# The beginning of each MLP: activations' forms made in steps beside the projection's last columns and the first products

## The chip, the cores and the metric

One core of one Trainium2 chip runs the whole program. TensorE (PE in the rows) does matmuls and transposes, VectorE (DVE) and ScalarE (ACT) the elementwise work, GpSimd (POOL) little here, and SyncE (SP) issues the loads of the weights. The metric is the device time of one execution in microseconds (us), the median of several runs.

## The reference

`x` has 256 tokens of width 2048. Everything is float32; the kernel gets that accuracy from TensorE by splitting each operand into a high and a low part.

```python
h = x
h = h + dsa_mixer(rmsnorm(h), a_w_in, a_w_out)        # top-64 keys of an indexer, then GQA; ends in "@ w_out"
h = h + sq_relu_mlp(rmsnorm(h, mlp_norm[0]), w_up[0], w_down[0])
k_sh, v_sh = shared K/V from rmsnorm(h, kv_norm) @ w_kv
h = h + dilated_mixer(rmsnorm(h), b_w_q, b_w_out, k_sh, v_sh)   # ends in "@ w_out" too
h = h + sq_relu_mlp(rmsnorm(h, mlp_norm[1]), w_up[1], w_down[1])
out = rmsnorm(h, final_norm)

def sq_relu_mlp(h, w_up, w_down):          # w_up 2048 x 8192, w_down 8192 x 2048
    u = jax.nn.relu(h @ w_up)
    return (u * u) @ w_down
```

## The kernel before

**Order of the program.** The kernel is a Python program that emits instructions for each engine; each engine runs its own in the order in which they were emitted or statically scheduled by the framework, and waits on semaphores where it needs another's result. Tiles come from pools with a fixed number of buffers; a new tile waits until the readers of the tile that had its buffer are through.

**A product.** Weights are loaded by `load_w` (L367) or `raws` (L699) as `wraw` tiles of 128 x 2 x 1024, one DMA of 1,024 KB each, issued in order on SP's queue. `split` (L190, L191) makes of each 1024 columns a high part `whi` (a cast on ScalarE) and a low part `wlo` (a subtraction on VectorE). TensorE then multiplies the activations' high part by both and their low part by the high part: three matmuls of 128 x 512 for each block (`gemm`, L389; `mm3`, L194 to L196). A step of `gemm` on 1024 columns is 12 such matmuls, after which `pump` takes some units from a queue of waiting work (generators handed over by `enqueue`); `flush` runs what is left.

**The projection.** `project` multiplies the heads' output by the second weight of the attention, in two column halves of 1024, and adds the result to the residual `h` (L652). The first `cut` of the 16 steps (8 in the first layer, 14 in the second) run for both halves while the last heads of attention are still finished beside them; then the `mlp` pool is opened, and the remaining steps run for each half in turn ("first columns", "second columns"), each with its own residual adds and the sums of squares for the norm (L331, ScalarE).

**The forms.** The MLP's first matrix product, `h @ w_up`, is computed block by block (`up(e)`, e from 0 to 7, 1024 columns each) as one 2 x 2 Strassen-like step with seven products on part of the depth and plain products on the rest. Its left operands are seven sums and differences of the activations' quarters (a11, a12, a22, s1 to s4), each split into high and low. `add_forms` makes them from `h`, half by half of the width: TensorE transposes `h` into a side bank (L299; there are two side banks), ScalarE copies and scales them (L307 for the plain part of half 0, L313 into a buffer `gx` that is taken from the weights' raw buffers), VectorE makes the low parts (L308) and sums (L316 to L319), and each form is split (L190, L191). It is called behind each half's columns:

```python
        for n in range(2):
            gemm(stat, range(cut, KC), w, 0, (n * GW, n * GW + HALF), residual(st, n))
            add_forms(forms, n, gain_next)
```

**The first block of the MLP.** `up(0)` loads two tiles of plain rows, computes two plain blocks (`plain(0, 0)`, `plain(0, 1)`), then three groups of seven products (`seven`), with two more plain blocks near the end. In a group of seven, VectorE also makes the weights' sums and differences in place, in the raw tiles (L731, L733, L735, L738). The results are combined from the eight accumulator banks (L746 to L765), and later transposed (L400) for the second matrix. During attention there are 3 raw, 4 high and 3 low weight buffers; the `mlp` pool adds 3 raw, 1 high and 2 low.

Of the kernel before, what the change touches and what calls it, by code (L numbers as in the profile page):

```python
# [11 lines left out]
F32 = mybir.dt.float32  # L12
# [80 lines left out]
def yoco_kernel(ctx: ExitStack, tc: tile.TileContext, x, a_w_in, a_w_out, w_kv, b_w_q, b_w_out, w_up, w_down,  # L93
# [13 lines left out]
    def open_scope(*names):  # L107
        if scope[0] is not None:
            scope[0].close()
        scope[0] = ExitStack()  # L110
        pools.clear()
        for n in names:
            pools[n] = scope[0].enter_context(tc.tile_pool(name=n, bufs=1))

    open_scope("keep", "att")
# [111 lines left out]

    def hi_lo():

        hi_of, lo_of = wp, wp  # L230
        if "mlp" in pools:
# [9 lines left out]
    def raw_tile():  # L241

        of = wp
        if "mlp" in pools:
# [46 lines left out]
    def add_forms(halves, half, which):  # L291
# [23 lines left out]
        s1, s2, s3, s4 = (b2()[:, :n * P].rearrange("p (q t) -> p q t", t=P) for _ in range(4))  # L315
        nc.vector.tensor_tensor(s1, a21, a22, op=ALU.add)  # L316
        nc.vector.tensor_tensor(s2, a11, s1, op=ALU.subtract)
        nc.vector.tensor_tensor(s3, a11, a21, op=ALU.subtract)
        nc.vector.tensor_tensor(s4, a12, s2, op=ALU.add)  # L319
        for name, v in (("a11", a11), ("a12", a12), ("s4", s4), ("s1", s1), ("s3", s3), ("s2", s2), ("a22", a22)):  # L320
            split(f[name][:, :, 0], f[name][:, :, 1], v)

# [48 lines left out]
    def gemm(stat, ks, w, row0, cols, evac, width=HALF, before=None, first_raw=None):  # L371
# [637 lines left out]
```

## Time and profile before

| | us |
|---|---|
| median of 3 runs | 2241.14 (2239.53 to 2241.89) |
| the profiled execution, its own time | 2240.57 |
| its span in the trace | 2238.6 |
| TensorE busy | 2176.6 |
| VectorE busy | 1692.6 |
| ScalarE busy | 1294.3 |

All stretches below are in microseconds from the start of the span. Rows of the table by stretches give the stretch, its length, the busy time of PE, PE's weight loads, DVE, ACT and POOL (each with the number of instructions), then the mean granted clock of TensorE as a share of full speed, the DMA engines' busy share and GB/s. Rows of the timeline give start, duration, engine, line, operation, out<-in with shape, the number of like instructions, and in brackets the idle time before them with what ended it. Rows of the waits give who waited for whom: total us, number of waits, the longest.

### The profile page before, as it was taken

The page shows a single profiled execution, that of the slowest core. Times are in us where ns is not written, and L with a number is a line of the kernel's source. Part 1 is how long each engine was busy: PE and PEld are TensorE (multiplying, and loading weights), DVE is VectorE, ACT ScalarE, POOL GpSimd, SP SyncE. Part 2 cuts the span into 40 slices and gives each one's busy share as a digit, 9 for nine tenths or more (in the row PEclk, how much of TensorE's full clock was granted, in tenths as well). Part 3 has the DMA queues.
Part 4 walks back from the last instruction along what each step waited for, and adds up shares of the span by engine and source line. Part 5 has one row for each costly group of instructions (what it writes and reads, how often), then busy time and mean ns, then how long its engine had stood idle before and what let it go on. Part 6 is the DMA issues. An engine that isn't in the chain of part 4 may idle for free.

```text
span 2238.6 us, 27840 instructions
## 1 busy us (share of the span) xinstructions
PE 2176.6 (97%) x10310; PEld 1792.3 (80%) x10310; DVE 1692.6 (76%) x2267; ACT 1294.3 (58%) x1736; POOL 99.5 (4%) x118
## 2 busy tenths in 40 slices
PE   9999988899999999999999999987999999999998
PEld 7788866688888888888888888865788888888886
DVE  5877749978878878866577777757979879779765
ACT  6545545656666666656455554445666666656563
POOL 0000000010010010110000000000010110100100
PEclk9999988999999999999999999998999999999999
DMA  8554534576676776674555445535477677777673
GB/s 301 162 178 150 162 139 146 174 226 227 207 231 224 208 225 238 206 244 136 173 163 162 156 156 162 185 121 181 164 222 248 194 228 241 207 226 242 204 250 95
DMA packets 164105, 434.44 MB, mean 194 GB/s; under 512 B 12800, under 2 KB 62080, under 8 KB 163968
## 3 DMA queue, kind: packets, MB, share of 16 engines
q1 hardware_dynamic: 146688, 401.25, 52.9%
q0 software_dynamic: 16128, 29.37, 7.4%
q10 hardware_dynamic: 1152, 2.04, 0.3%
q8 instruction: 81, 1.33, 0.2%
q14 instruction: 56, 0.46, 0.1%
HBM read 401.15 MB, written 2.10 MB: 180 GB/s over the span
## 4 chain that ended last, share of the span: by engine, by line
PE 90%; DVE 6%; ACT 2%; issue 1%; DMA 0%; DVEq 0%; ACTq 0%
PE acc L389 59%; PE acc L195 6%; PE acc L196 5%; PE acc L194 5%; PE side L195 4%; PE side L194 4%; PE side L196 4%; DVE wlo L191 2%; PE side L400 2%; ACT whi L190 1%; DVE wraw L733 1%; DVE wraw L735 0%; DMA wraw<-in_w_up_dram 0%; ACT b L331 0%; DVE wraw L731 0%
## 5 line engine op out<-in xcount | busy, mean ns | idle before, releaser
L190 ACT CAST whi<-wraw 128x1024 fp32r<-128x1024 f32 (+2 forms) x925 | 928.0, 1020 | 786.9 <-PE acc L389 510.1
L191 DVE TENSOR_TENSOR wlo<-wraw,whi 128x1024 fp32r<-128x1024 f32 (+2 forms) x925 | 1072.9, 1181 | 370.1 <-ACT whi L190 251.0
L389 PE MATMUL acc<-whi,xt 128*128 128x512 f32 x4160 | 1109.2, 380 | 7.7 <-ACT whi L190 7.7
L389 PEld LDWEIGHTS acc<-whi,xt 128*128 128x128 f32 x4160 | 739.7, 189 | 147.5 <-ACT whi L190 10.1
L389 PE MATMUL acc<-wlo,xt 128*128 128x512 f32 (+1 forms) x2080 | 619.2, 379 | 0.4 <-DVE wlo L191 0.4
L389 PEld LDWEIGHTS acc<-wlo,xt 128*128 128x128 f32 x2080 | 372.8, 188 | 75.4 <-DVE wlo L191 2.3
L649 POOL DMA_DIRECT2D h<-b x112 | 98.8, 1223 | 2094.1 <-ACT b L648 2076.0
L194 PE MATMUL side<-whi,xt 128*128 128x512 f32 x320 | 124.9, 400 | 15.2 <-ACT whi L190 14.4
L194 PE MATMUL acc<-whi,xt 128*128 128x512 f32 x328 | 129.3, 399 | 4.9 <-ACT whi L190 4.9
L195 PE MATMUL side<-wlo,xt 128*128 128x512 f32 x320 | 127.9, 400 | 0.8 <-DVE wlo L191 0.8
L195 PE MATMUL acc<-wlo,xt 128*128 128x512 f32 x328 | 127.9, 390 | 0.0
L196 PE MATMUL acc<-whi,xt 128*128 128x512 f32 x328 | 127.7, 389 | 0.0
L196 PE MATMUL side<-whi,xt 128*128 128x512 f32 x320 | 127.1, 397 | 0.0
L194 PE MATMUL acc<-whi,xf 128*128 128x512 f32 x288 | 114.9, 400 | 3.8 <-ACT whi L190 3.5
L195 PE MATMUL acc<-wlo,xf 128*128 128x512 f32 x288 | 115.0, 399 | 1.1 <-DVE wlo L191 1.1
L196 PE MATMUL acc<-whi,xf 128*128 128x512 f32 x288 | 112.9, 392 | 0.0
L194 PEld LDWEIGHTS side<-whi,xt 128*128 128x128 f32 x320 | 61.1, 192 | 30.7 <-ACT whi L190 16.9
L400 PE MATMUL side<-ident,b 128*128 128x128 f32 x512 | 77.1, 273 | 6.1 <-ACT b L773 4.9
L194 PEld LDWEIGHTS acc<-whi,xt 128*128 128x128 f32 x328 | 62.1, 190 | 22.1 <-ACT whi L190 9.8
L400 PEld LDWEIGHTS side<-ident,b 128*128 128x128 f32 x512 | 62.1, 140 | 21.4 <-ACT b L773 6.2
L195 PEld LDWEIGHTS side<-wlo,xt 128*128 128x128 f32 x320 | 61.6, 192 | 16.2 <-DVE wlo L191 2.0
L648 ACT ACTIVATE b<-acc,ri 128x512 f32<-128x512 f32 x112 | 71.0, 686 | 4.1
(194 smaller groups left out, 1738.3 us busy)
## 6 DMA issues: line engine op xcount, KB each, us to landing
wraw<-in_w_up_dram SPq DMA_DIRECT2D x128, 1024.0 KB, 6.4
wraw<-in_w_down_dram SPq DMA_DIRECT2D x128, 1024.0 KB, 6.6
wraw<-in_b_w_q_dram SPq DMA_DIRECT2D x192, 256.0 KB, 3.1
wraw<-in_a_w_in_dram SPq DMA_DIRECT2D x31, 1024.0 KB, 5.3
h<-b POOLq DMA_DIRECT2D x112, 256.0 KB, 7.7
wraw<-in_a_w_out_dram SPq DMA_DIRECT2D x16, 1024.0 KB, 5.7
wraw<-in_b_w_out_dram SPq DMA_DIRECT2D x16, 1024.0 KB, 5.5
wraw<-in_w_kv_dram SPq DMA_DIRECT2D x8, 1024.0 KB, 5.0
```

The lines of the kernel that those rows point to most:

```text
L190: nc.scalar.copy(hi, src)
L191: nc.vector.tensor_tensor(lo, src, hi.bitcast(F32), op=ALU.subtract)
L194: nc.tensor.matmul(o, a_hi, b_hi, start=start, stop=False)
L195: nc.tensor.matmul(o, a_hi, b_lo, start=False, stop=False)
L196: nc.tensor.matmul(o, a_lo, b_hi, start=False, stop=stop)
L389: nc.tensor.matmul(acc[t][i][:, :c1 - c0], stat(k, a, t), b[:, c0:c1], start=first and a == 0 and b is hi, stop=last and a == 1)
L400: nc.tensor.transpose(pt[:, j * P:(j + 1) * P], sr, ident)
L648: nc.scalar.activation(part, acc, AF.Copy, scale=scale()[:, t:t + 1])
L649: nc.gpsimd.dma_start(hh, part, accum_op=ALU.add)
L733: nc.vector.tensor_tensor(b12, b22, b12, op=sub)
```

## The change

`add_forms` becomes `form_steps`, which does nothing at once but returns two lists of steps: `on_pe` (transposes and copies) and `rest` (sums and splits). The sums come in another order, each followed by its split. `project` hands half 0's steps to the queue, spread over 8 steps of the second columns, so they are emitted between those columns' products; half 1's `on_pe` steps run behind the second columns, and its `rest` goes to the MLP as `late`, where the first group of seven of block 0 takes one step at each of its two hooks and the remaining ones behind it. `up(0)` runs three plain blocks ahead of the groups of seven, not two, and gives `q1` and `q6` the side banks. In the second layer (`again` is False) the cut is gone: the first columns run all 16 steps, with the heads finished (`heads_done`) before step 14, and the second columns run all 16 behind them. The residual adds run column by column. `gx` now always takes one of the `mlp` pool's 3 raw buffers, and the larger number of weight buffers (`more`) is used only from the start of `mlp` on.

```diff
-    def add_forms(halves, half, which):
+    def form_steps(halves, half, which):
...
-        if plain is not None:
-            for c in range(2):
-                for cc, pt, g in transposed(2 * half + c, 1):
-                    hi, lo = plain[:, 2 * c + cc - 2, 0, :], plain[:, 2 * c + cc - 2, 1, :]
-                    nc.scalar.activation(hi, pt, AF.Copy, scale=g)
-                    nc.vector.scalar_tensor_tensor(lo, pt, g, hi.bitcast(F32), op0=ALU.mult, op1=ALU.subtract)
-        gx = raw_tile()[:, :, :n * SEQ].rearrange("p c (j t) -> p c j t", t=SEQ)
-        for c in range(2):
-            for c2 in range(n // 2):
-                for cc, pt, g in transposed(2 * half + c, c2):
-                    nc.scalar.activation(gx[:, c, cc], pt, AF.Copy, scale=g)
+        gx = pools["mlp"].tile([P, 2, GW], F32, name="wraw", bufs=RAW_MORE)
+        gx = gx[:, :, :n * SEQ].rearrange("p c (j t) -> p c j t", t=SEQ)
...
+        def take(c, c2):
+            for cc, pt, g in transposed(2 * half + c, c2):
+                nc.scalar.activation(gx[:, c, cc], pt, AF.Copy, scale=g)
...
+        def sum_form(name, a, b, op):
+            a, b = (sums.get(v, v) if isinstance(v, str) else v for v in (a, b))
+            sums[name] = b2()[:, :n * P].rearrange("p (q t) -> p q t", t=P)
+            nc.vector.tensor_tensor(sums[name], a, b, op=op)
+            split_form(name, sums[name])
+
+        on_pe = [lambda c=c: split_plain(c) for c in range(2)] if plain is not None else []
+        on_pe += [lambda c=c, c2=c2: take(c, c2) for c in range(2) for c2 in range(n // 2)]
+        add, sub = ALU.add, ALU.subtract
+        rest = [lambda: split_form("a11", a11), lambda: split_form("a12", a12),
+                lambda: sum_form("s1", a21, a22, add), lambda: sum_form("s2", a11, "s1", sub),
+                lambda: sum_form("s4", a12, "s2", add), lambda: sum_form("s3", a11, a21, sub),
+                lambda: split_form("a22", a22)]
+        return on_pe, rest
...
-        for t in range(NT):
-            for i, (c0, c1) in enumerate(parts):
-                evac(t, i, acc[t][i][:, :c1 - c0])
+        ends = [(t, i) for t in range(NT) for i in range(len(parts))]
+        for t, i in sorted(ends, key=lambda ti: ti[1]) if by_column else ends:
+            evac(t, i, acc[t][i][:, :parts[i][1] - parts[i][0]])
...
+        def heads_done(k=cut):
+            if k == cut:
+                flush()
+                open_scope("mlp")
+                forms.extend(new_forms())
+
+        if again:
+            for n in range(2):
+                gemm(stat, range(cut), w, 0, cols[n], residual(None, n))
+            heads_done()
+            gemm(stat, range(cut, KC), w, 0, cols[0], residual(st, 0), by_column=True)
+        else:
+            gemm(stat, range(KC), w, 0, cols[0], residual(st, 0), before=heads_done, by_column=True)
+        on_pe, rest = form_steps(forms, 0, gain_next)
+        enqueue([(run(on_pe + rest), len(on_pe + rest))], 8)
+        gemm(stat, range(cut if again else 0, KC), w, 0, cols[1], residual(st, 1), by_column=True)
         flush()
...
+        on_pe, rest = form_steps(forms, 1, gain_next)
+        for step in on_pe:
+            step()
+        return st, forms, rest
...
+            if e == 0:
+
+                q5, q7, q2, q4, q3, q8 = (ps.tile([P, HALF], F32, name="acc") for _ in range(6))
+                q1, q6 = side(), side()
...
                 plain(0, 0)
                 plain(0, 1)
-                seven(0, 0)
+                plain(1, 0)
+                todo = run(late)
+                seven(0, 0, lambda: next(todo), lambda: next(todo))
+                for _ in todo:
+                    pass
                 seven(1, 0)
```

**First order rows: TensorE where the first layer's first columns end.** `acc` are accumulator banks, `side` the side banks, `xt` the heads' output, `whi` and `wlo` the split projection weight, `h` the residual. Before:

```order
L389 MATMUL acc<-wlo,xt 128x512 x2
L389 MATMUL acc<-whi,xt 128x512 x2
L299 MATMUL side<-ident,h_0_82 128x128
L299 MATMUL side<-ident,h_1_83 128x128
L299 MATMUL side<-ident,h_0_86 128x128
L299 MATMUL side<-ident,h_1_87 128x128
L299 MATMUL side<-ident,h_0_82 128x128
L299 MATMUL side<-ident,h_0_86 128x128
```

After:

```order
L410 MATMUL acc<-whi,xt 128x512 x2
L302 MATMUL side<-ident,h_0_82 128x128
L302 MATMUL side<-ident,h_0_86 128x128
L302 MATMUL side<-ident,h_1_83 128x128
L302 MATMUL side<-ident,h_1_87 128x128
L410 MATMUL acc<-whi,xt 128x512 x2
L410 MATMUL acc<-wlo,xt 128x512 x2
L410 MATMUL acc<-whi,xt 128x512 x3
L302 MATMUL side<-ident,h_0_82 128x128
L302 MATMUL side<-ident,h_0_86 128x128
L410 MATMUL acc<-whi,xt 128x512
L302 MATMUL side<-ident,h_1_83 128x128
```

Before, 16 transposes stand in one row, and no product stands between them; after, they stand in twos and fours between the second columns' products.

**Second order rows: VectorE in the second layer's first block, where half 1's forms end.** The numbers mark single tiles. `wraw_12952` (before) and `wraw_12936` (after) are `gx` of half 1, `xt`, `xf` and `b2` its forms and sums, the other `wraw` raw weights of `w_up`. Before:

```order
L191 TENSOR_TENSOR xf_12796<-b2_12982,xf_12796 128x4x128
L191 TENSOR_TENSOR xt_12795<-wraw_12952,xt_12795 128x4x128
L191 TENSOR_TENSOR wlo_13026<-wraw_13021,whi_13025 128x1024
L191 TENSOR_TENSOR wlo_13042<-wraw_13021,whi_13041 128x1024
L191 TENSOR_TENSOR wlo_13062<-wraw_13057,whi_13061 128x1024
```

After:

```order
L194 TENSOR_TENSOR wlo_13040<-wraw_13035,whi_13039 128x1024
L194 TENSOR_TENSOR xf_12548<-b2_13125,xf_12548 128x4x128
L775 TENSOR_TENSOR wraw_13035<-wraw_13035 128x2x512
L327 TENSOR_TENSOR b2_13129<-wraw_12936 128x512
L194 TENSOR_TENSOR xt_12547<-b2_13129,xt_12547 128x4x128
L777 TENSOR_TENSOR wraw_13035<-wraw_13037,wraw_13035 128x2x512
L194 TENSOR_TENSOR wlo_13051<-wraw_13037,whi_13050 128x1024
L194 TENSOR_TENSOR wlo_13062<-wraw_13037,whi_13061 128x1024
```

Before, all forms of half 1 stand ahead of the first plain block's split; after, the last of them stand among the first group of seven's splits and differences, and the last reader of `wraw_12936` is two instructions ahead of the first that reads `wraw_13037`, which takes its buffer.

**Third order rows: SP's loads at the beginning of the second layer's first block.** Before, the first two rows are the first group of seven's, which overtook the plain rows' (13021, 13023) in the schedule:

```order
L699 DMA wraw_13057<-in_w_up_dram 128x2x1024
L699 DMA wraw_13059<-in_w_up_dram 128x2x1024
L699 DMA wraw_13135<-in_w_up_dram 128x2x1024
L699 DMA wraw_13021<-in_w_up_dram 128x2x1024
L699 DMA wraw_13023<-in_w_up_dram 128x2x1024
```

After, the plain rows are 12983 and 12985, the first group of seven's 13035 and 13037:

```order
L743 DMA wraw_12983<-in_w_up_dram 128x2x1024
L743 DMA wraw_13135<-in_w_up_dram 128x2x1024
L743 DMA wraw_13137<-in_w_up_dram 128x2x1024
L743 DMA wraw_13213<-in_w_up_dram 128x2x1024
L743 DMA wraw_12985<-in_w_up_dram 128x2x1024
L743 DMA wraw_13035<-in_w_up_dram 128x2x1024
L743 DMA wraw_13037<-in_w_up_dram 128x2x1024
```

The loads of the first group of seven moved from the front to behind 13213, a load of the third group, whose buffer is that of 12983, the first plain rows.

## Rows read from the trace of the kernel before

**Rows 1.** The page, busy time and share of each engine

```profile
PE 2176.6 (97%) x10310; PEld 1792.3 (80%) x10310; DVE 1692.6 (76%) x2267; ACT 1294.3 (58%) x1736; POOL 99.5 (4%) x118
```

**Rows 2.** Busy time by stretch: both beginnings, front and rear; a steady stretch

```profile
294.40:330.60 36.20, 29.16 (x113) 21.84 (x112) 17.83 (x28) 17.59 (x35) 0.00 (x0) 0.81 0.41 146
330.60:395.50 64.90, 51.25 (x197) 37.46 (x195) 56.03 (x62) 39.16 (x55) 0.00 (x0) 0.87 0.42 145
1497.20:1516.20 19.00, 11.71 (x42) 7.60 (x41) 10.73 (x21) 10.44 (x27) 0.00 (x0) 0.73 0.36 125
1516.20:1581.00 64.80, 51.59 (x202) 38.07 (x200) 57.17 (x63) 39.81 (x56) 0.00 (x0) 0.87 0.49 174
...
500.00:570.00 70.00, 70.00 (x317) 57.57 (x316) 55.94 (x55) 42.45 (x50) 3.53 (x4) 1.00 0.73 241
```

**Rows 3.** Timeline of TensorE, first layer, from the first columns' end

```profile
294.47 0.38 PE L299 MATMUL side<-ident,h 128*128 128x128 f32 x2
...
305.81 0.80 PE L389 MATMUL acc<-whi,xt 128*128 128x512 f32 x1 [3.85 <-ACT whi L190]
...
330.61 0.38 PE L299 MATMUL side<-ident,h 128*128 128x128 f32 x2
```

**Rows 4.** Waits, first layer, 285 to 430: total us, times, longest

```profile
PE side L194 <- ACT whi L190: 7.1, 3, 3.2
...
PE acc L389 <- ACT whi L190: 3.9, 1, 3.9
PE side L299 <- ACT wraw L313: 3.7, 6, 1.1
...
PE side L299 <- DVE xt L308: 1.2, 2, 0.7
...
PE side L299 <- DVE h L652: 0.9, 3, 0.3
```

**Rows 5.** Timeline of TensorE, second layer, the same two places

```profile
1497.30 0.38 PE L299 MATMUL side<-ident,h 128*128 128x128 f32 x2
...
1516.27 0.38 PE L299 MATMUL side<-ident,h 128*128 128x128 f32 x2
```

**Rows 6.** Waits of VectorE, 330.6 to 395.5

```profile
DVE wraw L733 <- DMA wraw<-in_w_up_dram: 2.7, 1, 2.7
DVE xt L191 <- ACT xt L190: 2.3, 1, 2.3
```

**Rows 7.** Chain that ended last, 285 to 430: start, duration, what

```profile
284.88 8.17 PE acc L389 x36
...
371.69 4.92 DMA wraw<-in_w_up_dram
```

**Rows 8.** Timeline of TensorE at full clock, a transposed block

```profile
394.02 0.60 PE L400 MATMUL side<-ident,b 128*128 128x128 f32 x4
394.37 0.48 PE L194 MATMUL acc<-whi,xt 128*128 128x512 f32 x1
```

**Rows 9.** Timeline of VectorE and ScalarE: splits of weights and of forms

```profile
305.96 5.76 DVE L191 TENSOR_TENSOR wlo<-wraw,whi 128x1024 fp32r<-128x1024 f32 x5
...
328.09 1.05 ACT L190 CAST whi<-wraw 128x1024 fp32r<-128x1024 f32 x1 [9.82 <-PE acc L389]
...
341.24 0.69 DVE L191 TENSOR_TENSOR xt<-b,xt 128x512 fp32r<-128x512 f32 x1
341.85 1.29 DVE L191 TENSOR_TENSOR xf<-b,xf 128x512 fp32r<-128x512 f32 x2
```

**Rows 10.** Loads of w_up, 1480 to 1590: us from issue to landing

```profile
DMA to landing us min/median/max: 4.9/5.2/10.5
```

**Rows 11.** Timeline of SP's queue: the first layer's loads of w_up

```profile
310.62 57.91 SPq L699 DMA_DIRECT2D wraw<-in_w_up_dram  x10
```

**Rows 12.** Timeline of TensorE: products that start at its low clock

```profile
345.95 0.63 PE L195 MATMUL side<-wlo,xt 128*128 128x512 f32 x1
346.38 0.63 PE L196 MATMUL side<-whi,xt 128*128 128x512 f32 x1
```

More of the change, by code (lines that the diff above doesn't have):

```diff
@@ L109, in open_scope @@
             scope[0].close()
+        more[0] = False
         scope[0] = ExitStack()
@@ L113, in open_scope @@
             pools[n] = scope[0].enter_context(tc.tile_pool(name=n, bufs=1))
+    more = [False]
     open_scope("keep", "att")
@@ L230, in hi_lo @@
         hi_of, lo_of = wp, wp
-        if "mlp" in pools:
+        if more[0]:
             hi_of = wp if turn[0] < HI_BUFS else pools["mlp"]
@@ L243, in raw_tile @@
         of = wp
-        if "mlp" in pools:
+        if more[0]:
             of = wp if raw_turn[0] < RAW_BUFS else pools["mlp"]
@@ new lines, in form_steps, with split_plain @@
+        sums = {}
+        def split_plain(c):
+            for cc, pt, g in transposed(2 * half + c, 1):
+                hi, lo = plain[:, 2 * c + cc - 2, 0, :], plain[:, 2 * c + cc - 2, 1, :]
+                nc.scalar.activation(hi, pt, AF.Copy, scale=g)
+                nc.vector.scalar_tensor_tensor(lo, pt, g, hi.bitcast(F32), op0=ALU.mult, op1=ALU.subtract)
+        def take(c, c2):
+            for cc, pt, g in transposed(2 * half + c, c2):
+                nc.scalar.activation(gx[:, c, cc], pt, AF.Copy, scale=g)
@@ L323, in yoco_kernel, with run @@
+        add, sub = ALU.add, ALU.subtract
[4 more added lines that the diff above has]
+        return on_pe, rest
+    def run(steps):
+        for step in steps:
+            step()
+            yield
     class Stats:
@@ L369, in load_w, with gemm @@
         return raw
-    def gemm(stat, ks, w, row0, cols, evac, width=HALF, before=None, first_raw=None):
+    def gemm(stat, ks, w, row0, cols, evac, width=HALF, before=None, first_raw=None, by_column=False):
         wd = len(cols) * width
@@ L657, in residual, with project, mlp @@
         return evac
-    def project(oTs, w, gain_next, cut):
+    def project(oTs, w, gain_next, cut, again):
         st = Stats()
         stat = stat_of(oTs)
-        for n in range(2):
-            gemm(stat, range(cut), w, 0, (n * GW, n * GW + HALF), residual(None, n))
-        flush()
-        open_scope("mlp")
-        forms = new_forms()
-        for n in range(2):
-            gemm(stat, range(cut, KC), w, 0, (n * GW, n * GW + HALF), residual(st, n))
-            add_forms(forms, n, gain_next)
-        return st, forms
-    st, xm = project(oTs, a_w_out[0], G_M0, CUT_A)
+        cols = [(n * GW, n * GW + HALF) for n in range(2)]
+        forms = []
+        def heads_done(k=cut):
[13 more added lines that the diff above has]
+        gemm(stat, range(cut if again else 0, KC), w, 0, cols[1], residual(st, 1), by_column=True)
+        flush()
+        on_pe, rest = form_steps(forms, 1, gain_next)
+        for step in on_pe:
+            step()
+        return st, forms, rest
+    st, xm, late = project(oTs, a_w_out[0], G_M0, CUT_A, True)
     NE = DFF // GW
-    def mlp(i, xm, st_in, gains_next, final=None):
+    def mlp(i, xm, late, st_in, gains_next, final=None):
         us = {}
+        more[0] = True
         r2 = st_in.inv_square()
         def up(e):
-            q1, q6, q5, q7, q3, q8 = (ps.tile([P, HALF], F32, name="acc") for _ in range(6))
-            q2, q4 = side(), side()
+            if e == 0:
+                q5, q7, q2, q4, q3, q8 = (ps.tile([P, HALF], F32, name="acc") for _ in range(6))
+                q1, q6 = side(), side()
+            else:
+                q1, q6, q5, q7, q3, q8 = (ps.tile([P, HALF], F32, name="acc") for _ in range(6))
+                q2, q4 = side(), side()
             banks = dict(q1=q1, q2=q2, q3=q3, q4=q4, q5=q5, q6=q6, q7=q7, q8=q8)
@@ L744, in nearly_done @@
             def nearly_done():
-                plain(1, 0)
+                if e:
+                    plain(1, 0)
                 nc.scalar.copy(c11, q1)
@@ L754, in up @@
                 plain(0, 1)
-                seven(0, 0)
+                plain(1, 0)
+                todo = run(late)
+                seven(0, 0, lambda: next(todo), lambda: next(todo))
+                for _ in todo:
+                    pass
                 seven(1, 0)
@@ L804, in mlp @@
         final(stat_of([us.pop(2 * NE - 2), us.pop(2 * NE - 1)]), w_down[i], (NE - 1) * GW, r2)
-    st, (xkv, xq) = mlp(0, xm, st, [G_KV, G_B])
+    st, (xkv, xq) = mlp(0, xm, late, st, [G_KV, G_B])
     open_scope("keep", "att")
@@ L971, in final @@
         finish(1)
-    mlp(1, xm, st, [], final)
+    mlp(1, xm, late, st, [], final)
     scope[0].close()
```

9 lines of the change are left out of this document (2 added, 7 removed).

## The prediction

> **What bounds the kernel now.** The page comes first: TensorE is busy 97% of the span, VectorE 76% [rows 1]. That average hides the only place where TensorE really waits inside the span. The table by stretches shows it [rows 2]: in the steady middle of an MLP (500 to 570 us, all such stretches alike) TensorE is busy for all of its 70 us, at full clock. At the beginning of the MLPs it is not. I call the first MLP's beginning A and the second's B, and split each at the end of the projection's second columns: front part (A 294.4 to 330.6, B 1497.2 to 1516.2) and rear part, the MLP's first block (A to 395.5, B to 1581.0). In the front parts TensorE is busy 29.2 of 36.2 and 11.7 of 19.0 us at a mean clock of 0.81 and 0.73.
>
> The timeline of TensorE then says why [rows 3]. At 294.47 the first columns' products are done and the 16 transposes of half 0 begin; the next product starts at 305.81, after waiting 3.85 us for ScalarE. Between these, each pair of transposes waits for ScalarE and VectorE to empty the two side banks [rows 4]. The list of waits puts 3.9 us on that product, 7.1 on the MLP's first products and 3.7 on transposes waiting for ScalarE's copies. B repeats A to within 0.2 us: 1497.30 to 1516.27 [rows 5].
>
> In the rear parts VectorE is the bound, not TensorE: busy 56.0 of 64.9 us and 57.2 of 64.8 [rows 2]. Its idle time there (8.9 and 7.6) is in few pieces: in A 2.7 us for a load of w_up and 2.3 for ScalarE's first split of half 1 [rows 6]. So a gain in front is a shift of the rear part's start, and a gain in the rear is only what shortens VectorE's queue.
>
> **The change, part by part.**
>
> *Half 0's forms beside the second columns (front).* Removed: the stop of TensorE. What stays in its queue is the same work: 16 transposes, and the products, 8 steps of 12 in A and 2 steps of 12 that lie in this stretch in B. A product costs 0.227 us (36 in 8.17) [rows 7], a transpose 0.09 in a full-clock row (4 in 0.35, from the start of the four to the start of the next product) [rows 8]. The transposes now stand in pairs between the products of the second columns (first order rows), and some pairs still wait for the pair before to be copied out. By the static order: the first four follow 12 products (2.7 us), in which VectorE's residual adds are done; ScalarE then has four squares and two weight casts ahead of its first copy, so the second, third and fourth pairs come 0.2 to 0.5 us early. I take 1.3 us for A and 1.0 for B. The bounds: nothing if products cover all of it, and 2.9, half of what both halves' transposes waited for all reasons in A (3.7 + 1.2 + 0.9, the last two by the same list) [rows 4].
>
> A: 96 x 0.227 + 16 x 0.09 + 1.3 = 24.5 us instead of 36.1: **11.6**. B: 24 x 0.227 + 1.4 + 1.0 = 7.8, and 0.5 more because the last heads of attention must now be finished before step 14 of the first columns instead of beside the second columns' steps; their tail stands between products, so I take 0.5 of the at most 2.7 that one step of cover is worth: 8.3 instead of 19.0, **10.7**. What hides the forms' work on ScalarE and VectorE is the second columns' products; VectorE has 17.8 us of work in A's 36.2 [rows 2], and needs it all plus two splits (below) within 24.5. Without that cover the 11 us come back.
>
> *Edits at nothing.* In B the second set of residual adds (8 instructions of VectorE) disappears, off the path. The other order of residuals, the exchange of banks in block 0, and three plain blocks ahead change no amount of work. The second columns run with 3 raw, 4 high and 3 low buffers where they had 6, 5 and 5 in their last part; two steps of products last 5.4 us and a lone load 4.9 [rows 7], three buffers ahead, so I cost this at nothing; if a load came a whole length late it would cost 5 us.
>
> *Half 1's forms beside the first products (rear).* VectorE's work is the same, less two low-part splits of the plain blocks that it can now do before the second columns end: 2 x 1.13 = 2.3 (five in 5.76, less the 0.1 by which an instruction overlaps the next: one of 0.69 is followed after 0.61) [rows 9]. So only its idle time can change. The forms still begin with the chain square, copy, transpose, copy through ScalarE; walking the order I get 3.1 us of idle in A (0.2 for a low buffer, 1.3 and 1.6 for ScalarE) and 5.0 in B, where the third plain block's split stands behind the forms.
>
> Then a wait that the change adds: each half's copy lies in an MLP weight buffer. The next load into half 1's buffer can start only when VectorE has read it for the last time. In A that is the second load of the second group of seven; behind the last read stand two short splits of 0.60, a split of 1.13 and a difference, counted alike [rows 9], then the split that needs the load. A lone load takes 4.92 [rows 7], a cast on ScalarE 1.05 [rows 9]: 4.92 + 1.05 - 3.5 = 2.5, with issue 2.7. In B it is the second load of the first group of seven, and only one split of 0.60 stands between (second order rows): 4.92 - 0.6 + 0.2 = 4.5. The whole rest of the block is queued behind that instruction on VectorE, and TensorE waits for it. Bounds: 0 if the forms finish while other work is queued, and 10.5, the slowest landing of a w_up load there [rows 10]; I take 4.92 because it is the row with nothing else in flight, as here.
>
> The Trainium skill, page "DMA: Bandwidth & Descriptors", section on the anatomy of one DMA, fits a copy as about 2.0 us plus its bytes over 436 GB/s, for copies issued by GpSimd; for 1,024 KB that is an estimate of 4.4 us. By it both waits are 0.5 us shorter and the total 2212.0. No w_up load here landed in less than 4.9 [rows 10], so the rows' price stands.
>
> A: 56.0 - 2.3 + (3.1 + 2.7) = 59.5 instead of 64.9: **5.4**. B: 57.2 - 2.3 + (5.0 + 4.5) = 64.4 instead of 64.8: **0.4**.
>
> Sum: 11.6 + 10.7 + 5.4 + 0.4 = 28.1. The profiled execution took 2240.57 us (span 2238.6), the median of the runs is 2241.14, 0.57 more: 2240.57 - 28.1 + 0.57 = **2213.0**. After block 0 nothing differs but buffer turns, and TensorE is the bound there.
>
> **The rivals.**
>
> *Loads hold the rear back.* On SP's queue the loads of the first group of seven now stand behind one that waits for the first plain blocks (third order rows); if they and the two late loads land at 10.5 instead of 4.92 [rows 10], each rear loses about 5.6, and A's plain blocks no longer cover the first: 28.1 - 11.2 - 3 = 14, so 2227. For it: five loads at once are what made the slow landings. Against: the plain blocks give TensorE 36 products, 8.2 us of cover.
>
> *The stalls are smaller than I walked.* No front waits (2.3 + 0.5) and half of the 7.2 us at the two loads: 6.4 more, 2206.6. Against it: VectorE runs its queue in order, and the loads cannot start earlier.
>
> *Nothing comes through.* The front gets shorter but the rear starts from the weights, not from the second columns' end: 2240. This would need w_up loads that come no earlier than before; but before, SP issued them from 310.62 on, 20 us ahead of the rear [rows 11], and they move with the buffers.
>
> *Slower.* The second columns are now cut by short waits, in A for 8 steps and in B for 16. If the granted clock fell to 1.2 GHz there, each product would take 0.43 us (two starts at the low level, 345.95 and 346.38) [rows 12], 0.20 more: 288 products, 58 us. It decides against the change from 28.1 / 0.20 = 140 such products on; with all, 2271. For it: in both front parts the mean clock is below full already [rows 2]. Against: it fell there only after TensorE had stood through waits of 3 to 4 us and ten of little else [rows 3, 4], and none of the new waits is above 0.5.
> The Trainium skill, page "TensorE: Matmul & The Clock Gate", section "A second HAM failure mode", says that frequent short idles between groups of matmuls can alone make the clock swing. No row here shows that: in the steady stretch with all its interleaved transposes the clock is 1.00.
>
> **How the numbers follow.** My forecast, 2213 with its bounds 2207 to 2221: 0.70. Smaller stalls, below 2207: 0.10. Late loads, 2221 to 2234: 0.13. Nothing: 0.03. Slower: 0.04. Leaving out the lowest tail and the last two, the range is 2204 to 2228. A measurement of this kernel tells about 0.2% (4.5 us) from no change: faster 0.93, same 0.03, slower 0.04.
>
> **What would show it.** In the profile after: between the first columns' last product and the second columns' last, about 24.5 us in A at a clock of 1.00, 16 transposes with waits below 0.6; the gap of 3.85 gone. In the rear, VectorE idle about 3 and 2.7 us in A, 5 and 4.5 in B, the second of each at a wait of the row difference or split for a w_up load; block 0 from 64.9 to about 59.5 in A and unchanged in B. I am wrong if TensorE's clock in the second columns is below 0.95, if the loads' waits exceed 6 us, or if the steady stretch grows idle.

## The result and the profile after

The changed kernel takes 2212.17 us (2211.91 to 2216.02, 4 runs) where the kernel before takes 2241.36; the ratio is 0.9875, with a 95% interval of 0.9858 to 0.9892. The forecast was 2213.0 with a range of 2204 to 2228. The total is right, but it is a sum of five pieces, and one of them was not in the forecast.

The table by stretches of the changed kernel: front and rear of the first layer's beginning, then of the second's (columns as in [rows 2]). The second layer's front row covers all of its second columns, since half 0's transposes stand at their beginning now (1441.34 to 1448.24).

```profile
294.40:318.30 23.90, 23.90 (x114) 19.59 (x113) 17.62 (x29) 16.68 (x33) 0.00 (x0) 1.00 0.54 178
318.30:374.20 55.90, 48.01 (x198) 34.54 (x195) 53.49 (x60) 36.82 (x53) 0.00 (x0) 0.97 0.57 200
1440.90:1484.30 43.40, 43.40 (x200) 35.34 (x198) 25.04 (x34) 21.66 (x35) 0.00 (x0) 1.00 0.63 207
1484.20:1548.00 63.80, 49.69 (x202) 35.37 (x200) 54.45 (x60) 36.54 (x53) 0.00 (x0) 0.95 0.47 165
```

TensorE now has no gap at all in either front part, and its clock is at its upper level (1.00) there. The rear parts are 55.9 us instead of 64.9, and 63.8 instead of 64.8 [rows 2]. The timeline of TensorE shows the transposes between the products, and where the second columns end in each layer:

```profile
297.26 0.60 PE L302 MATMUL side<-ident,h 128*128 128x128 f32 x4
297.61 0.71 PE L410 MATMUL acc<-whi,xt 128*128 128x512 f32 x2
...
318.38 0.38 PE L302 MATMUL side<-ident,h 128*128 128x128 f32 x2
...
1484.30 0.38 PE L302 MATMUL side<-ident,h 128*128 128x128 f32 x2
```

They answer to 330.61 [rows 3] and 1516.27 [rows 5]. To see how the gain builds up, take instructions that both kernels have in equal number, and compare when the first or the last of them starts. Before (the first adds by DMA, in the first MLP; the last scores of the second attention; the last transposes of the second MLP):

```profile
L649 POOL DMA_DIRECT2D h<-b x112: 859/1200/1945, 468.7 to 2193.0; - x112
L842 PE MATMUL side<-kT,b3r x48: 277/282/335, 1134.6 to 1434.9; 128*128 128x256 f32 x48
L400 PE MATMUL side<-ident,b x512: 270/272/421, 63.8 to 2158.6; 128*128 128x128 f32 x171
```

After (durations are minimum, median and maximum in ns, then first and last start in us):

```profile
L670 POOL DMA_DIRECT2D h<-b x112: 862/1260/1942, 447.4 to 2159.1; - x112
L891 PE MATMUL side<-kT,b3r x48: 277/282/335, 1113.9 to 1414.1; 128*128 128x256 f32 x48
L421 PE MATMUL side<-ident,b x512: 270/272/476, 64.0 to 2125.3; 128*128 128x128 f32 x171
```

| checkpoint | before | after | ahead by | so this stretch gives | forecast |
|---|---|---|---|---|---|
| end of the second columns, first layer | 330.61 | 318.38 | 12.2 | 12.2 | 11.6 |
| first adds of the first MLP | 468.7 | 447.4 | 21.3 | 9.1 | 5.4 |
| last scores of the second attention | 1434.9 | 1414.1 | 20.8 | -0.5 | 0 |
| end of the second columns, second layer | 1516.27 | 1484.30 | 32.0 | 11.2 | 10.7 |
| last transposes of the second MLP | 2158.6 | 2125.3 | 33.3 | 1.3 | 0.4 |
| end of the span | 2238.6 | 2210.0 | 28.6 | -4.7 | 0 |

The last line is the surprise: 33 us ahead, the kernel loses 4.7 in its last 85 us. ScalarE's timeline there, after:

```profile
2154.53 1.04 ACT L193 CAST xt<-wraw 128x1024 fp32r<-128x1024 f32 x1 [2.15 <-DMA wraw<-in_w_down_dram]
2155.48 1.04 ACT L193 CAST whi<-wraw 128x1024 fp32r<-128x1024 f32 x1
2156.43 2.42 ACT L669 ACTIVATE b<-acc,ri 128x512 f32<-128x512 f32 x4
```

and TensorE's, which waits for these evacuations to get its next accumulator banks:

```profile
2157.16 1.08 PE L410 MATMUL acc<-whi,xt 128*128 128x512 f32 x2 [2.95 <-ACT b L669]
...
2158.55 1.78 PE L410 MATMUL acc<-whi,xt 128*128 128x512 f32 x4
```

The wait is 2.95 of the 4.7 us. Behind it four products take 1.78 us, where four ahead of it take 1.07: the mean granted clock from 2153 to 2163 is 0.83 (1.00 in the kernel before, from 2186.3 to 2191.4).

Before, two of the four evacuations (L648) stand ahead of that cast:

```profile
2186.47 1.24 ACT L648 ACTIVATE b<-acc,ri 128x512 f32<-128x512 f32 x2
2190.51 1.05 ACT L190 CAST xt<-wraw 128x1024 fp32r<-128x1024 f32 x1 [2.80 <-DMA wraw<-in_w_down_dram]
```

The cast waits for a load of the last weights in both. After, all four evacuations are queued behind it; before, two were through already.

The waits of VectorE in the two rear parts, first layer and second:

```profile
DVE b L327 <- ACT wraw L319: 1.1, 1, 1.1
DVE xt L194 <- ACT xt L193: 1.1, 1, 1.1
```

```profile
DVE wraw L777 <- DMA wraw<-in_w_up_dram: 3.6, 1, 3.6
DVE xt L194 <- ACT xt L193: 3.0, 2, 1.9
DVE rv L356 <- ACT b L352: 1.4, 1, 1.4
DVE b L327 <- ACT wraw L319: 1.1, 1, 1.1
```

The load wait that the forecast put into both layers is there in the second only.

### The profile page after: what moved, and what is told of

It is laid out like the page before. It is cut to its first block, busy times and chain, and to the rows that moved or that the text cites. A ratio compares the mean times of both kernels' runs of the same rounds, so it can differ in the third digit from the quotient of the medians.

```text
span 2210.0 us, 27845 instructions
## 1 busy us (share of the span) xinstructions
PE 2163.2 (98%) x10310; PEld 1784.1 (81%) x10310; DVE 1687.7 (76%) x2259; ACT 1293.9 (59%) x1736; POOL 99.7 (5%) x118
## 3 DMA queue, kind: packets, MB, share of 16 engines
q1 hardware_dynamic: 146688, 401.25, 53.5%
## 4 chain that ended last, share of the span: by engine, by line
PE 90%; DVE 6%; ACT 2%; DMA 1%; issue 1%; DVEq 0%; ACTq 0%
PE acc L410 59%; PE acc L198 6%; PE acc L197 5%; PE acc L199 5%; PE side L197 4%; PE side L199 3%; PE side L198 3%; DVE wlo L194 3%; PE side L421 2%; ACT whi L193 1%; DMA wraw<-in_w_down_dram 1%; DVE wraw L779 1%; DVE wraw L777 0%; DMA wraw<-in_w_up_dram 0%; DVE wraw L775 0%
## 5 line engine op out<-in xcount | busy, mean ns | idle before, releaser
L410 PE MATMUL acc<-whi,xt 128*128 128x512 f32 x4160 | 1110.7, 380 | 3.8 <-ACT b L669 2.9
L410 PEld LDWEIGHTS acc<-whi,xt 128*128 128x128 f32 x4160 | 738.3, 188 | 141.9 <-ACT b L669 3.8
L410 PEld LDWEIGHTS acc<-wlo,xt 128*128 128x128 f32 x2080 | 372.3, 188 | 75.0 <-DVE wlo L194 1.9
L197 PE MATMUL acc<-whi,xt 128*128 128x512 f32 x356 | 140.8, 398 | 13.2 <-ACT whi L193 13.2
L198 PE MATMUL acc<-wlo,xt 128*128 128x512 f32 x356 | 140.1, 394 | 1.0 <-DVE wlo L194 0.9
L199 PE MATMUL acc<-whi,xt 128*128 128x512 f32 x356 | 139.6, 392 | 0.0
L198 PE MATMUL side<-wlo,xt 128*128 128x512 f32 x292 | 114.9, 394 | 3.5 <-DVE wlo L194 3.3
L197 PE MATMUL acc<-whi,xf 128*128 128x512 f32 x276 | 110.0, 399 | 5.8 <-ACT whi L193 5.5
L199 PE MATMUL side<-whi,xt 128*128 128x512 f32 x292 | 114.7, 393 | 0.0
L197 PE MATMUL side<-whi,xt 128*128 128x512 f32 x292 | 111.9, 392 | 0.0
L198 PE MATMUL acc<-wlo,xf 128*128 128x512 f32 x276 | 109.4, 396 | 0.9 <-DVE wlo L194 0.9
L199 PE MATMUL acc<-whi,xf 128*128 128x512 f32 x276 | 107.8, 391 | 0.0
L197 PEld LDWEIGHTS acc<-whi,xt 128*128 128x128 f32 x356 | 67.1, 189 | 32.9 <-ACT whi L193 19.8
L198 PEld LDWEIGHTS acc<-wlo,xt 128*128 128x128 f32 x356 | 67.1, 188 | 15.8 <-DVE wlo L194 2.5
L199 PEld LDWEIGHTS acc<-whi,xt 128*128 128x128 f32 x356 | 67.1, 189 | 13.7
```

The lines of the kernel that those rows point to most:

```text
L197: nc.tensor.matmul(o, a_hi, b_hi, start=start, stop=False)
L198: nc.tensor.matmul(o, a_hi, b_lo, start=False, stop=False)
L199: nc.tensor.matmul(o, a_lo, b_hi, start=False, stop=stop)
L410: nc.tensor.matmul(acc[t][i][:, :c1 - c0], stat(k, a, t), b[:, c0:c1], start=first and a == 0 and b is hi, stop=last and a == 1)
```

## The experiments

The kernel before has a median of 2240.9 to 2241.6 us beside these runs. Two profiles of the same code can differ by some 2 us: in the experiment that changes the second layer's cut alone, the first layer's first adds start at 449.5 and not at 447.4. Differences of that size in one profile are not read as effects below.

### What ended TensorE's stop

**Half 0's forms in one piece again.**

```diff
-        enqueue([(run(on_pe + rest), len(on_pe + rest))], 8)
+        for step in on_pe + rest:
+            step()
```

> The changed kernel, with half 0's forms made in one piece between the first and the second columns, as before the change; all else as changed. Theory (the front gains come from the interleaving alone): the first layer loses 12.2 us, the second 11.2: 2212.2 + 23.4 = 2235.6. Rival (the other edits of the front, the residual adds by column and the cut that is gone, carry a part): below 2225.

Measured: 2214.23 us (2213.95 to 2215.0; ratio 0.9877, 0.986 to 0.9893). That is 2.1 more than the changed kernel, not 23.4. The timeline of TensorE at the start of the second columns:

```profile
294.97 0.38 PE L302 MATMUL side<-ident,h 128*128 128x128 f32 x2
295.10 0.71 PE L410 MATMUL acc<-whi,xt 128*128 128x512 f32 x2
```

The forms are written in one piece, and the static schedule mixes them with the products all the same. So the steps are not needed to remove the stop, and the theory that I gave there falls. The time lies on its rival's side (below 2225), but the rival names the residual adds by column and the cut, and the third of the next experiments does without both. What else the change does in front of this place is in the buffers, so three experiments start from the kernel before.

**The weight buffers' number alone.**

```diff
-        if "mlp" in pools:
+        if more[0]:          # True from the start of mlp on; in hi_lo and raw_tile
```

> The kernel before, with one edit of the change alone: the larger number of weight buffers is used only from the start of the MLP on (3 raw, 4 high, 3 low during the projection). Theory (what ends TensorE's stop is that the copy of half 0 no longer shares a pool with the second columns' weights; with this edit alone it still does, now in the smaller pool, and the 16 transposes still stand in one row): 2241 within 5, the stop of some 11 us in both layers unchanged. Rival (the larger pools, opened late, are themselves the cause): 2225 or less.

Measured: 2241.59 us (ratio 1.0006, 0.9996 to 1.0015): no change in the total. The stop is there, with the same wait at its end, and this edit alone already puts the cast ahead of all four evacuations at the end:

```profile
306.78 1.22 PE L390 MATMUL acc<-whi,xt 128*128 128x512 f32 x2 [3.85 <-ACT whi L190]
...
L401 PE MATMUL side<-ident,b x512: 269/272/474, 65.5 to 2156.4; 128*128 128x128 f32 x171
...
2186.00 1.04 ACT L190 CAST xt<-wraw 128x1024 fp32r<-128x1024 f32 x1 [2.62 <-DMA wraw<-in_w_down_dram]
...
2187.90 2.41 ACT L649 ACTIVATE b<-acc,ri 128x512 f32<-128x512 f32 x4
```

From the last transposes to the end of its span (2241.7) it takes 85.3 us, as the changed kernel does (84.7), where the kernel before takes 80.0. Since the median is unchanged with an end that is 5.3 longer, some 5 us must be gained ahead of it; in this profile, whose execution is 2.0 above the median, 2.2 of them are seen at the last transposes (2156.4 for 2158.6). So the unchanged total hides a gain and the loss at the end.

**The copies' buffers alone.**

```diff
-        gx = raw_tile()[:, :, :n * SEQ].rearrange("p c (j t) -> p c j t", t=SEQ)
+        gx = pools["mlp"].tile([P, 2, GW], F32, name="wraw", bufs=RAW_MORE)
+        gx = gx[:, :, :n * SEQ].rearrange("p c (j t) -> p c j t", t=SEQ)
```

> The kernel before, with the other buffer edit alone: the copies of both halves in the MLP's raw buffers, with the larger number of weight buffers during the projection as before. Theory (both edits are needed: here the second columns' first load still comes from the pool that the copy is in, and the 16 transposes still stand in one row): 2241 within 5. Rival (this edit alone frees the second columns' casts): 2225 or less.

Measured: 2229.66 us (ratio 0.9945, 0.993 to 0.996), between the two, which neither the theory nor the rival gives. The timeline says that the theory holds for the stop and that the time is from elsewhere:

```profile
305.58 0.80 PE L390 MATMUL acc<-whi,xt 128*128 128x512 f32 x1 [3.85 <-ACT whi L190]
```

The stop stands as before (305.81 in [rows 3]), in the second layer too; what this kernel gains lies behind it: at the checkpoints above, 4.1 us up to the first adds of the first MLP and 7.6 from the last scores to the last transposes, with 79.8 us at the end. There the copies no longer take a turn among the raw buffers; that part was not taken further apart.

**Both buffer edits.** The two diffs above together, nothing else of the change.

> The kernel before, with the change's two edits of the buffers alone: the larger number of weight buffers only from the start of the MLP on, and the copies of both halves in the MLP's raw buffers, apart from the projection's weights. The forms are still written in one piece behind each half's columns, there are two plain blocks, the old banks and the old cut in the second layer. Theory (the buffers' pools alone let the schedule mix the transposes between the products): the first layer loses 2.5 us against the changed kernel (1.3 each, as the two experiments that undid its steps showed), the second 0 to 3: 2214 to 2218. Rival 1 (handing over the forms in steps is what does it): 2235 to 2241. Rival 2 (the first layer gains, but with the old cut the second columns of the second layer, two steps of 2.7 us, cannot hold the forms): 2222 to 2226.

Measured: 2216.4 us (2214.4 to 2217.54; ratio 0.9887, 0.9871 to 0.9904): the theory's value, and 24.5 of the change's 29.2 us. The timeline of TensorE:

```profile
294.86 0.38 PE L300 MATMUL side<-ident,h 128*128 128x128 f32 x2
295.00 0.71 PE L391 MATMUL acc<-whi,xt 128*128 128x512 f32 x2
```

In the second layer TensorE is busy for all of 1440 to 1486 us as well. So, with the forms in one piece, the stop ends when the projection's weights and the copy of half 0 come from pools of their own, and with neither edit alone. Whether the steps in the old buffers would end it too was not run. Before, both take turns over the six buffers of the two pools, and with the smaller number alone both take turns in the weights' own three. The order of ScalarE before shows what that did (2686 is the copy, 2727 the second columns' first load):

```
L190 CAST xt_2510<-wraw_2686 128x2x128
...
L190 CAST whi_2729<-wraw_2727 128x1024
L190 CAST whi_2745<-wraw_2727 128x1024
L190 CAST whi_2763<-wraw_2761 128x1024
```

All casts of the second columns stand behind the forms. The timeline of ScalarE before and the loads of the projection's weights from 255 us on add that it had the time and the weights for them earlier:

```profile
293.80 0.63 ACT L331 ACTIVATE b<-h 128x512 f32<-128x512 f32 x1 [11.64 <-DVE h L652]
...
304.72 4.83 ACT L190 CAST whi<-wraw 128x1024 fp32r<-128x1024 f32 x5
...
L367 SPq DMA_DIRECT2D wraw<-in_a_w_out_dram x7: 367/367/722, 255.9 to 278.9; - x7
DMA to landing us min/median/max: 5.2/6.6/10.1
```

It idled for 11.64 us until 293.80, did the forms, and then made five casts in a row, for which TensorE waited. The last of the loads had been issued at 278.9 and none took more than 10.1 us, so all weights were there by 289.0: the stop is the order of ScalarE and not a late load. That the schedule hands out a pool's tiles in the program's order, so that a weight behind the copy gets its place late, fits these runs but is argued, not shown.

**The old cut in the second layer.**

```diff
-    st, xm, late = project(oTs, b_w_out[0], G_M1, CUT_B, False)
+    st, xm, late = project(oTs, b_w_out[0], G_M1, CUT_B, True)
```

> The changed kernel, with the old cut in the second layer: only the last two steps of each half's columns run behind the end of the heads. Theory (two steps, 24 products and 5.4 us, do not hold half 0's forms, so the rest of them stands ahead of the first block's splits on VectorE): 5 to 8 us slower than the changed kernel, 2217 to 2220. Rival 1 (the cover is not needed, since the scheduler hides the forms elsewhere): 2211 to 2213. Rival 2 (the prediction's price: the heads' tail costs 0.5 us when the cut goes, so with the cut kept it is 0.5 faster): 2211.7.

Measured: 2215.55 us (2214.01 to 2216.77; ratio 0.9886, 0.9871 to 0.9901), 3.4 more than the changed kernel. The direction is the theory's, the size below it; neither rival holds. In the trace the last transposes of the second MLP start at 2130.0:

```profile
L891 PE MATMUL side<-kT,b3r x48: 278/283/336, 1115.2 to 1415.5; 128*128 128x256 f32 x48
L421 PE MATMUL side<-ident,b x512: 269/272/477, 64.0 to 2130.0; 128*128 128x128 f32 x171
```

They are 4.7 behind the changed kernel, of which 1.4 stood already at the last scores: 3.3 are the second layer's. Two steps of cover do not hold the forms: of half 0's 16 transposes eight stand within the second columns, the other eight behind them (from 1484.39), between the first block's products.

### The rear, and the load that waits

**The rear of before.** Half 1's sums and splits run at once behind its copies, two plain blocks, the old banks:

```diff
-        for step in on_pe:
+        for step in on_pe + rest:
             step()
-        return st, forms, rest
+        return st, forms, []
...
-                plain(1, 0)
                 todo = run(late)
```

> The changed kernel, with the rear as before the change: half 1's sums and splits run at once behind its copies, two plain blocks ahead, the banks of before. Theory (the rear's gains come from the rear's edits): the first layer loses 9.1 us, the second 1.0: 2222.3. Rival 1 (a part of the first layer's 9.1 comes from the new front, which hands over a full clock and weights that are split already): 2212.2 + 5.4 + 0.4 = 2218, the rear's price in the prediction. Rival 2 (late forms give nothing): 2212 to 2214.

Measured: 2212.5 us (2212.03 to 2213.01; ratio 0.9868, 0.9854 to 0.9883): no difference to the changed kernel. Rival 2 holds. The rear's edits give nothing, and the 9.1 us that the first layer's rear gained must have come with the front and its buffers. The rear part of this kernel in the first layer, in the columns of [rows 2]:

```profile
319.00:376.00 57.00, 48.55 (x195) 34.43 (x194) 53.02 (x60) 36.67 (x52) 0.00 (x0) 0.97 0.55 196
```

VectorE is idle for 4.0 of 57.0 us, where it was for 8.9 of 64.9 before.

**Half 1's copy out of the raw buffers.** It goes into the activations' pool, where the heads' output has just come free:

```diff
-        gx = pools["mlp"].tile([P, 2, GW], F32, name="wraw", bufs=RAW_MORE)
+        if half == 0:
+            gx = pools["mlp"].tile([P, 2, GW], F32, name="wraw", bufs=RAW_MORE)
+        else:
+            gx = xtp.tile([P, 2, GW], F32, name="gx", tag="xt")
```

> The changed kernel, with half 1's copy of the activations in a buffer of the activations' pool and not in one of the MLP's raw weight buffers, so that no load of w_up waits for its last reader. Theory (the wait of 3.6 us at the second layer's first row difference is that load, and VectorE sets the end there): 2212.2 - 3.6 = 2208.6, all of it in the second layer. Rival 1 (nothing to gain, because TensorE or ScalarE ends last there anyway): 2212. Rival 2 (five loads in flight slow each other, so another load comes late): 2210 to 2213 with a new wait on a load of w_up.

Measured: 2197.95 us (2196.67 to 2198.95; ratio 0.9803, 0.9789 to 0.9818), 14.2 less than the changed kernel, where 3.6 was expected. The mechanism is right and its size is not: the second layer's rear is 52.5 us now.

```profile
1484.50:1537.00 52.50, 44.32 (x191) 33.15 (x189) 52.34 (x59) 34.69 (x51) 0.00 (x0) 1.00 0.41 140
```

VectorE is idle for 0.2 us in it, where the changed kernel has 9.4 (63.80 - 54.45). The wait of 3.6 was only the part that carries the load's name. With the buffer free, the first group's weights are there before the forms (their first difference starts at 1484.66, where the changed kernel has it at 1498.42), so their splits and differences fill VectorE's other waits, for ScalarE's squares (1.4 above) and its part of the forms (3.0 and 1.1), as well.

### The end

**The last casts behind the evacuations.**

```diff
-                nc.scalar.activation(part, acc, AF.Copy, scale=scale()[:, t:t + 1])
+                emptied[0] = nc.scalar.activation(part, acc, AF.Copy, scale=scale()[:, t:t + 1])
...
-            split(*ws[k], raw[:, k % 2])
+            with tc.issue_after(emptied[0].ins) if k >= 4 else nullcontext():
+                split(*ws[k], raw[:, k % 2])
```

> The changed kernel, with one order forced at its end: on ScalarE, the casts of the last weights (steps 4 and up of the last product) are issued behind the four evacuations of the product before, of which the first stood behind a cast that waits for a load. Theory (the 4.9 us that the changed kernel loses against the gain it had at 2137 us come from that order): 2212.2 - 4.9 = 2207.3. Rival (the load itself is late, and TensorE then waits for the cast and split instead): 2212 still, with a wait of 3 to 5 us at the last product's third pair of steps.

Measured: 2208.33 us (2207.91 to 2209.04; ratio 0.985, 0.9835 to 0.9865), 3.8 less, where 4.9 was expected. The theory holds: ScalarE evacuates without a wait, TensorE has no wait from 2140 to 2180, and the end from the last transposes on takes 79.9 us, as before the change (80.0).

```profile
2154.22 2.39 ACT L671 ACTIVATE b<-acc,ri 128x512 f32<-128x512 f32 x4
```

**The raw buffers' turn of before, in the second MLP.**

```diff
         more[0] = True
+        raw_turn[0] = (raw_turn[0] + 2 * i) % (RAW_BUFS + RAW_MORE)
```

> The changed kernel, with the turn of the raw weight buffers moved on by two at the start of the second MLP, which gives the turn that the kernel before had there; no order is forced. In the order the cast of the last product's third load then stands behind two of the four evacuations, as before the change. Theory (the turn of the buffers, shifted by two because the copies no longer take a turn in the second layer, is what put that cast ahead): 4 to 5 us less at the end, 2207 to 2208.5, if the first block of the second layer keeps its loads in time. Rival (the turn has nothing to do with it, the end stalls as before): 2212.

Measured: 2213.15 us (2212.82 to 2215.19; ratio 0.9875, 0.9859 to 0.9892), so by the time alone the rival. The trace tells two effects apart that cancel:

```profile
L892 PE MATMUL side<-kT,b3r x48: 277/283/335, 1114.2 to 1414.5; 128*128 128x256 f32 x48
L421 PE MATMUL side<-ident,b x512: 270/272/473, 64.2 to 2131.2; 128*128 128x128 f32 x171
```

It comes to the last transposes 5.9 us behind the changed kernel, 5.5 of which it loses behind the second attention, and its span is only 1.0 us longer (2211.0). So the end gives back 4.9, and the reason is seen on ScalarE, with two evacuations ahead of the cast again:

```profile
2159.17 1.26 ACT L669 ACTIVATE b<-acc,ri 128x512 f32<-128x512 f32 x2
2162.88 1.05 ACT L193 CAST xt<-wraw 128x1024 fp32r<-128x1024 f32 x1 [2.46 <-DMA wraw<-in_w_down_dram]
```

The turn of the buffers sets the order at the end, as the theory says. What moved it is the smaller number of buffers during the projection, and not the copies alone: the end takes 85.3 us with that edit alone and 79.8 with the copies' buffers alone. The second MLP's first block pays for the turn of before: half 1's transposes stand in one row again, and the first product behind them starts at 1494.69, where the changed kernel has products between the transposes from 1484.43 on.

```profile
1494.69 2.17 PE L197 MATMUL acc<-whi,xt 128*128 128x512 f32 x4 [2.68 <-ACT whi L193]
```

### The versions that beat both

**Half 1's copy in the activations' pool, and the forced order at the end.**

> Both improvements on the changed kernel together: half 1's copy in the activations' pool, and the last casts issued behind the evacuations. Theory (they are at different places and add up): 2197.95 - 3.9 to 4.7 = 2193.2 to 2194.1. Rival (the new buffers change the turns, so the end had another stall than the one that the order removes): 2198.

Measured: 2194.06 us (2193.64 to 2195.24; ratio 0.9791, 0.9777 to 0.9806). They add up.

**The same on the kernel before with the buffer edits, without steps, new cut, late forms or third plain block.**

> The kernel before, with buffers and the end's order alone: the two buffer edits, half 1's copy in the activations' pool, the last casts behind the evacuations; no steps, no new cut, two plain blocks, old banks. Theory 1 (once the forms hide, the buffers carry nearly everything): 2216.4 - 4.5 for the end, and up to 9 for the second layer's first block: 2203 to 2206. Theory 2 (with the old cut the second columns of the second layer are too short, and the loads of the first group of seven stay behind one that waits): 2210 to 2212.

Measured: 2206.48 us (2205.57 to 2208.07; ratio 0.9843, 0.9829 to 0.9858), just outside theory 1 and better than theory 2. It beats the change as it was made, with a few lines, but is 12 to 14 behind the best: what it leaves out in front (steps, residual adds by column, the sums' order and the new cut) is worth more once the rear's loads are free. Without that freedom the same was worth 3.9 (2216.4 to 2212.5).

**The best with the rear of before.**

> The best version so far (2194.1) with the rear of before: half 1's sums and splits at once behind its copies, two plain blocks ahead, the banks of before. Theory (with the load wait gone VectorE works through in either order, and the rear's edits are worth little): 2194 to 2198. Rival (the late forms and the third plain block keep TensorE fed while VectorE makes the forms, and only show now): 2202 or more.

Measured: 2192.89 us (2192.34 to 2194.17; ratio 0.9783, 0.9768 to 0.9797): the theory, 1.1 below its range. The two best differ by 1.2 us, and the simpler rear is not the slower one.

```profile
1483.50:1536.00 52.50, 46.14 (x197) 33.79 (x195) 52.15 (x59) 35.35 (x53) 0.00 (x0) 1.00 0.40 140
```

VectorE is busy for 52.15 of the second layer's 52.5 us in the rear, so what bounds this block now is VectorE's own work.

## Why the prediction was right

**Front, right in size, wrong in cause.** 12.2 and 11.2 us against 11.6 and 10.7. The price of a product held. For a transpose the first layer leaves 0.13 us ((23.9 - 96 x 0.227) / 16) where 0.09 was taken, and the waits that I added (1.3 and 1.0) did not come, since TensorE has no idle time in either stretch. (That B repeats A to within 0.2 us was misread, and no term uses it: from the first transpose to the next product it is 11.3 us in A and 10.8 in B.) But the step that put the gain down to the transposes "between the products of the second columns (first order rows)" took the order for the work of the steps. Written in one piece the forms cost 2.1 us, and the two buffer edits alone bring the mixed order: what ended the stop is that the second columns' casts no longer stand behind the forms on ScalarE. The prediction names these edits only under "Edits at nothing" (fewer raw, high and low buffers) and as a wait that they add.

**First rear, mis-sized.** 9.1 us against 5.4. VectorE's work came out as forecast (53.5 us; 56.0 - 2.3 = 53.7), its idle time at 2.4 and not 5.8. The failed step is "in A that is the second load of the second group of seven". The trace shows that load issued at 338.57, when the first group's last split ends (337.33 + 1.21), and another at 341.58, when the last sum that reads the copy ends (340.88 + 0.68):

```profile
338.57 0.37 SPq L743 DMA_DIRECT2D wraw<-in_w_up_dram  x1
341.58 0.37 SPq L743 DMA_DIRECT2D wraw<-in_w_up_dram  x1
```

```profile
337.33 1.21 DVE L194 TENSOR_TENSOR wlo<-wraw,whi 128x1024 fp32r<-128x1024 f32 x1
...
340.88 0.68 DVE L327 TENSOR_TENSOR b<-wraw 128x512 f32<-128x512 f32 x1
```

The load behind the copy is one of the next block's, which nobody waits for. The wait that was priced there is 2.7 of the 3.4 us of idle time that did not come. I had the buffers handed out in turn; here they go to whichever load comes next.

**Second rear, right.** 1.0 us by the stretches, against 0.4. The load wait is at the difference that the second order rows point to, 3.6 us against 4.5; VectorE's idle time is 9.4 against 9.5. The price of that wait was stated as if it stood alone, and the experiment shows that 11.3 us of the block hung on the copy's buffer (63.8 to 52.5).

**The end, missed.** The failed step is "After block 0 nothing differs but buffer turns, and TensorE is the bound there". The turns decide the order of ScalarE at the end, and that order cost 4.7 us. The total came out right by luck: this loss and the first rear's extra gain of 3.7 nearly cancel.

**The rivals.** *The stalls are smaller than I walked* is nearest in its parts: no front waits, and one of the two waits at loads is gone. Without the loss at the end the kernel takes 2208.33, between that rival's 2206.6 and the forecast. For *Loads hold the rear back* the row was misread: "five loads at once are what made the slow landings", but the 10.5 is the slowest of four, issued from 1508.4 to 1511.6. The slower one, a lower clock from short waits between products, has no ground: the second columns run at 1.00 in both layers, with 16 transposes among them. The sentence of the Trainium skill, page "TensorE: Matmul & The Clock Gate", section "A second HAM failure mode", was not put to the test, because the idles that it speaks of did not occur. By the Trainium skill, page "DMA: Bandwidth & Descriptors", section on the anatomy of one DMA, whose fit is for copies issued by GpSimd, the estimate for a lone load was 4.4 us; the loads of w_up in the first layer, which SyncE issues, landed in no less than 4.8 after the change, so the measured price stands:

```profile
DMA to landing us min/median/max: 4.8/5.1/9.0
```

## What to carry to other kernels

When a schedule is made statically, buffers that are shared between a prefetch and a copy can hold work back like a dependency: look for idle time of the engine that feeds the stop, ahead of the stop, before writing code in another order. Price a buffer that a load waits for by the whole queue behind it, not by the wait that the list shows; moving one copy to a pool that had room was worth half as much as the entire change. And compare both kernels at checkpoints through the whole program, since a total that fits can be the sum of two errors, and a total that does not move can be a gain and a loss.

## What was not expected of the hardware

In the first layer's second columns, 16 transposes of 128 x 128 in twos and fours stood between 96 products, and TensorE was busy for all of 23.9 us at a granted clock of 1.00; before, the same work with a stop took 36.2 us at a mean of 0.81 [rows 2]. Behind it the first layer's rear ran at 0.87 before and at 0.97 after.
